# Output projections of a two-layer decoder trunk as seven block products, their block sums on GpSimd

## The chip, the core and the metric

The kernel runs on one core of a Trainium2 chip. A core has engines that run side by side, each with its own queue of instructions: TensorE (PE in the profile; its weight loads are the rows PEld) multiplies matrices, VectorE (DVE), ScalarE (ACT) and GpSimd (POOL) work element by element, and SyncE (SP) issues most of the transfers. An engine takes its instructions strictly in order; one that waits for a semaphore holds up all that stand behind it. SBUF is the on-chip memory of 128 partitions, PSUM the accumulator memory into which TensorE writes. The metric is the device time of one execution, in microseconds (us); lower is better.

## The reference

Two layers run over a sequence of 1024 positions, model width 1024, all in float32. Each has a token mixer (multi-head latent attention in layer 0, sliding-window attention in layer 1) beside four memory cross-attention heads, then one output projection, then a squared-ReLU MLP:

```python
def reference(x, mem, positions, ...):
    mem_n = rmsnorm(mem, mem_norm_g)
    for i in range(DEPTH):                       # DEPTH = 2
        hn = rmsnorm(x, attn_norm_g[i])
        if i % 2 == 0:
            mix, q_cross = mla_mixer(hn, positions, ...)      # 12 heads of 64
        else:
            mix, q_cross = swa_mixer(hn, positions, ...)      # 12 heads of 64
        cross = memory_cross_attention(q_cross, mem_n, w_mem_kv[i])   # 4 heads of 64
        x = x + jnp.concatenate([mix, cross], axis=-1) @ w_o[i]       # 1024x1024 @ 1024x1024
        x = x + squared_relu_mlp(rmsnorm(x, mlp_norm_g[i]), mlp_w_up[i], mlp_w_down[i])
    return rmsnorm(x, final_norm_g)
```

The line that ends in `@ w_o[i]` is what the change is about: a product of two 1024 x 1024 matrices in each layer, added to the residual `x`, whose row-wise RMS norm then feeds the MLP.

## The kernel before, in words

**Numbers.** Products are made of pairs: a float32 operand is split into a high part, which ScalarE copies with rounding (line 99), and a low part, the difference, which VectorE subtracts (line 100). A product of two such operands is three matmuls, high by high, high by low and low by high (`mm3`, lines 108 to 110). So each operand that TensorE is to use costs one ScalarE and one VectorE instruction first. A matmul takes a 128x128 block of stationary weights and 512 columns.

**The output projection.** `wo_phase` runs once in each layer, between the attention and the MLP. It works in two halves, output columns 0 to 511 and then 512 to 1023, and in each through eight tiles of 128 rows. A tile is eight 128-deep steps of three matmuls, 24 in all, into one PSUM bank `pswo`; so a layer has 2 x 8 x 24 = 384 of these matmuls. `WoHalf` loads and splits the weights of a half (`woq` of the first, `g` of the second), and `o_split` splits one row tile of the attention's output ahead of its use. The order is written out in the code: each engine gets its instructions in the order in which a tile's turn issues them, and a scheduler moves some of them by its own estimate of readiness.

**Behind each tile.** VectorE adds the bank to the residual (line 1294, one per tile and half). In the second half each tile is then stored to `xd` by two transfers on GpSimd's queue (line 1303), normed (`norm`: the squares on ScalarE at line 1150, five small operations on VectorE from line 1154 to 1159, then the scaled halves, one on ScalarE at line 1230 and one on VectorE at line 1231) and transposed by TensorE (`xT_`, line 1241) one tile later, between two tiles' matmuls. The transposed tile is split or copied for the MLP. For tiles 4 to 7 four subtractions on VectorE (lines 1248 to 1251) make the block combinations that the MLP needs, since both products of the MLP use the seven-product scheme already.

**Around it.** In layer 0 the attention's last head is divided by its sums in `last_o`: four reciprocals and four products on VectorE (lines 986 and 987) for each half of the rows. For rows 0 to 511 they are dealt out between the first four tiles. In layer 1 the sliding-window attention normalises its weights with GpSimd (line 1996). `fill_w` makes the first weights of the MLP: it scales them by the norm's gain on ScalarE, 128x128 at a time (line 1320), and splits them. In the MLP the matmuls that come first are named `psu` and `psv` (lines 1421 to 1423).

## Time and profile before

| what | value |
|---|---|
| median of 3 runs | 2111.34 us (2109.48 to 2112.94) |
| the profiled execution's own time | 2109.36 us |
| its span, first to last instruction | 2107.5 us |
| mean granted clock of TensorE | 0.999 |
| busy share PE, DVE, ACT, POOL | 99%, 70%, 53%, 7% |
| output projection of layer 0 | begins at 442.8 us, the MLP's first matmul at 538.3 us |
| output projection of layer 1 | begins at 1392.4 us, the MLP's first matmul at 1486.2 us |

The page of a profile gives busy times and shares, then groups of equal instructions. A row of the timeline is read as: start, duration, engine, line of the source, operation, written tile, read tiles, and in brackets how long the engine had been idle and what ended that. Two rows of one engine can overlap by about 0.1 us, since an instruction begins while the one ahead still drains; what an instruction costs in a full queue is the distance between two starts. Times in all parts are positions within this one execution.

### The profile page before, as it was taken

The page shows a single profiled execution, that of the slowest core. Times are in us where ns is not written, and L with a number is a line of the kernel's source. Part 1 is how long each engine was busy: PE and PEld are TensorE (multiplying, and loading weights), DVE is VectorE, ACT ScalarE, POOL GpSimd, SP SyncE. Part 2 cuts the span into 40 slices and gives each one's busy share as a digit, 9 for nine tenths or more (in the row PEclk, how much of TensorE's full clock was granted, in tenths as well). Part 3 has the DMA queues.
Part 4 walks back from the last instruction along what each step waited for, and adds up shares of the span by engine and source line. Part 5 has one row for each costly group of instructions (what it writes and reads, how often), then busy time and mean ns, then how long its engine had stood idle before and what let it go on. Part 6 is the DMA issues. An engine that isn't in the chain of part 4 may idle for free.

```text
span 2107.5 us, 28961 instructions
## 1 busy us (share of the span) xinstructions
PE 2082.1 (99%) x9830; PEld 1691.0 (80%) x9830; DVE 1476.6 (70%) x2929; ACT 1114.6 (53%) x2408; POOL 147.9 (7%) x248
## 2 busy tenths in 40 slices
PE   8999999999999999999999999999999999999998
PEld 7888766678888888888888878778788888888887
DVE  8766677775977776976557535666977776976565
ACT  7554466656755444444445435776755444444453
POOL 1001001010000000000001133420000000000000
PEclk9999999999999999999999999999999999999999
DMA  6202223343355446954433634542345446844342
GB/s 237 79 1 76 63 64 92 91 136 100 112 169 165 152 143 231 321 152 156 136 119 103 153 90 126 140 136 85 111 164 165 159 141 231 318 150 154 119 120 88
DMA packets 180756, 292.34 MB, mean 139 GB/s; under 512 B 16659, under 2 KB 70784, under 8 KB 180608
## 3 DMA queue, kind: packets, MB, share of 16 engines
q1 hardware_dynamic: 174096, 272.07, 41.4%
q0 software_dynamic: 5200, 15.80, 2.1%
q10 hardware_dynamic: 1312, 2.63, 0.4%
q8 instruction: 77, 1.26, 0.3%
q14 instruction: 71, 0.58, 0.1%
HBM read 187.34 MB, written 81.18 MB: 127 GB/s over the span
## 4 chain that ended last, share of the span: by engine, by line
PE 90%; DVE 5%; DMA 2%; ACT 2%; issue 1%; SPq 0%; DVEq 0%; ACTq 0%
PE psy L1730 5%; PE psy L1728 5%; PE psy L1729 5%; PE psu L1421 5%; PE psu L1422 5%; PE psu L1423 5%; PE psz L1728 4%; PE psz L1730 4%; PE psz L1729 4%; PE psv L1422 4%; PE psv L1421 4%; PE psv L1423 4%; PE pso L947 4%; PE pss L917 3%; PE pswo L108 3%; PE pswo L110 3%
## 5 line engine op out<-in xcount | busy, mean ns | idle before, releaser
L927 ACT ACTIVATE p<-pss 128x512 f32<-128x512 f32 (+2 forms) x144 | 68.7, 487 | 69.2 <-DVE pss L925 52.5
L1728 PE MATMUL psy<-g 128*128 128x512 f32 x256 | 99.9, 390 | 0.0
L1729 PE MATMUL psy<-g 128*128 128x512 f32 x256 | 99.6, 389 | 0.0
L1730 PE MATMUL psy<-g 128*128 128x512 f32 x256 | 99.4, 390 | 0.0
L99 ACT ACTIVATE g<-i 128x512 fp32r<-128x512 f32 x79 | 49.7, 629 | 92.5 <-PE psz L1729 46.0
L100 DVE TENSOR_TENSOR g<-i,g 128x512 fp32r<-128x512 f32 x79 | 55.6, 704 | 47.6 <-ACT g L99 47.6
L99 ACT ACTIVATE i<-mr 128x512 fp32r<-128x512 f32 x78 | 47.8, 628 | 74.0 <-PE psy L1729 25.6
L796 DVE TENSOR_REDUCE m<-psx 128x1 f32<-128x1024 f32 (+7 forms) x96 | 72.0, 752 | 20.1 <-PE psx L795 19.7
L99 ACT ACTIVATE uh<-i 128x512 fp32r<-128x512 f32 x66 | 41.7, 631 | 83.9 <-PE psy L1729 39.5
L947 PE MATMUL pso<-p,vf 128*128 128x512 f32 (+2 forms) x192 | 85.4, 527 | 0.6 <-ACT p L927 0.6
L100 DVE TENSOR_TENSOR uh<-i,uh 128x512 fp32r<-128x512 f32 x66 | 45.6, 690 | 46.8 <-ACT uh L99 46.6
L1728 PE MATMUL psz<-g 128*128 128x512 f32 x192 | 74.7, 389 | 0.0
L1729 PE MATMUL psz<-g 128*128 128x512 f32 x192 | 74.7, 389 | 0.0
L1730 PE MATMUL psz<-g 128*128 128x512 f32 x192 | 74.7, 389 | 0.0
L1320 ACT ACTIVATE mr<-mr,gcol 128x256 f32<-128x256 f32 (+1 forms) x160 | 63.9, 475 | 13.5 <-DMA mr<-in_mlp_w_up_dram 13.5
L100 DVE TENSOR_TENSOR i<-mr,i 128x512 fp32r<-128x512 f32 x78 | 53.6, 687 | 21.5 <-ACT i L99 21.5
L917 PE MATMUL pss<-qh,kh 97*128 97x512 f32 (+2 forms) x144 | 67.9, 474 | 0.0
L917 PE MATMUL pss<-ql,kh 97*128 97x512 f32 (+2 forms) x144 | 58.2, 404 | 0.0
L1641 DVE TENSOR_TENSOR mqf<-mqq,mqf 128x512 f32<-128x512 f32 x64 | 43.4, 688 | 20.6 <-DMA mqq<-in_mlp_w_down_dram 20.3
L1730 PEld LDWEIGHTS psy<-g 128*128 128x128 f32 x256 | 48.1, 188 | 10.0
L1729 PEld LDWEIGHTS psy<-g 128*128 128x128 f32 x256 | 48.1, 188 | 9.9
L1728 PEld LDWEIGHTS psy<-g 128*128 128x128 f32 x256 | 48.1, 188 | 9.8
(658 smaller groups left out, 6862.2 us busy)
## 6 DMA issues: line engine op xcount, KB each, us to landing
i<-hd SPq DMA_DIRECT2D x154, 256.0 KB
hd<-uh SPq DMA_DIRECT2D x76, 256.0 KB
hd<-ul SPq DMA_DIRECT2D x76, 256.0 KB
mr<-in_mlp_w_up_dram SPq DMA_DIRECT2D x36, 512.0 KB
hd<-x SPq DMA_DIRECT2D x72, 256.0 KB
mr<-hd SPq DMA_DIRECT2D x70, 256.0 KB
d<-in_mlp_w_up_dram SPq DMA_DIRECT2D x32, 512.0 KB
mqq<-in_mlp_w_down_dram SPq DMA_DIRECT2D x32, 512.0 KB
```

The lines of the kernel that those rows point to most:

```text
L99: nc.scalar.activation(hi, src, AF.Copy)
L100: nc.vector.tensor_tensor(lo, src, f32(hi), ALU.subtract)
L796: nc.vector.reduce_max(m8s[h][:, i : i + 1], ps[:, :n], axis=AX, negate=True)
L917: return lambda: nc.tensor.matmul(o, a, b, skip_group_check=True, **kw)
L927: nc.scalar.activation(p[:, c0:], ps, AF.Exp, scale=SC)
L947: mms.append(lambda: nc.tensor.matmul(o, a, b, skip_group_check=True, **kw))
L1421: nc.tensor.matmul(ps, wh[:, k, :], xh[:, k, :], start=p in (1, 2, 5) and k == 0, stop=False, skip_group_check=True)
L1422: nc.tensor.matmul(ps, wh[:, k, :], xl[:, k, :], start=False, stop=False, skip_group_check=True)
L1423: nc.tensor.matmul(ps, wl[:, k, :], xh[:, k, :], start=False, stop=k == 3, skip_group_check=True)
L1728: nc.tensor.matmul(ps, ah[:, j, :], bh, start=p in (1, 5, 2) and k == 0, stop=False, skip_group_check=True)
L1729: nc.tensor.matmul(ps, ah[:, j, :], bl, start=False, stop=False, skip_group_check=True)
L1730: nc.tensor.matmul(ps, al[:, j, :], bh, start=False, stop=k == NP - 1, skip_group_check=True)
```

## The change

A class `Wo` takes the place of `WoHalf`. The attention output A (rows by heads) and the weights B are cut into 2 x 2 blocks of 512: A12 is rows 0 to 511 by the early heads, B21 the weights of the early heads by columns 0 to 511, and so on. Seven block products are made in the order 2, 1, 5, 6, 3, 7, 4:

```text
P2 = A12 B21            P5 = (A21+A22) (B12-B11)     P6 = (A21+A22-A11) (B22-B12+B11)
P1 = A11 B11            P3 = (A12-A21-A22+A11) B22   P7 = (A11-A21) (B22-B12)
P4 = A22 (B21-B22+B12-B11)
```

Each is 4 row tiles x 4 steps x 3 = 48 matmuls. Some products continue in a bank (6 and 7 on top of 1; 3 on top of 5), and VectorE adds the banks to four residual blocks `a1`, `u2`, `c21`, `a5` of 512 x 512 (line 1324 of the new source): 36 additions in a layer, where there were 16.

Every product needs four A blocks and four B blocks of 128x512 split anew, into a ring of eight operand sets (`set_`). The sums and differences of blocks are GpSimd instructions of 128x512 (`sums`, lines 765 to 776): 8 for P5, 8 for P6, 4 for P3, 8 for P7 and 4 for P4, 32 in a layer. Also given to GpSimd are one half of the norm's scaling (line 1293, 8 in a layer, ScalarE before), the gain scaling in `fill_w` (line 1400, 2 of 128x1024 in a layer for 16 small ones on ScalarE) and the subtractions for tiles 4, 5 and 6 (lines 1312 to 1315, 12 in a layer; tile 7's stay on VectorE).

P2 needs the early heads only, and its matmuls are put among the last steps of the attention, in eight pieces of six (`first`). In layer 0 `last_o` for rows 0 to 511 is issued whole, ahead of P1's operands. Residuals and weights come in transfers of 1 MB, and the four result blocks leave in one transfer each on SyncE's queue, where there were 32 smaller ones on GpSimd's. Rows 0 to 511 are complete when P3 is added, so their norms stand among P3 and P7 and their transposes among P7; rows 512 to 1023 are complete with P4, the last product, so the norms of tiles 4 to 7 follow P4's tiles, and the transposes of tiles 6 and 7 stand in the MLP's first product.

**GpSimd's queue, layer 0.** Before, it had only the issues of transfers here (`xd` is the result in DRAM, `i..` the tiles), then, much later, a weight scaling of the next layer. The last three of those issues and what follows:

```order
L1303 DMA xd_4796<-i32_0_49_5320 128x512
L1303 DMA xd_4796<-i30_0_53_5382 128x512
L1303 DMA xd_4796<-i31_0_60_5458 128x512
L1841 TENSOR_TENSOR wsr1_9773<-wsr1_9773,gcol_73 128x1024
L1699 DMA x1_4795<-d2_0_152_7966 128x512 x2
```

Now the stretch holds the sums (`ul` and `uh` are the sum blocks of A and B, `fa1` and `qn0` the attention's output, `x0`, `x1`, `x2` the weight blocks B12, B22, B21). From the second half of P7's sums to the subtractions of tile 4 the rows run:

```order
L773 TENSOR_TENSOR fa1_87<-fa1_87 128x512
L774 TENSOR_TENSOR x0_0_2_4883<-x1_0_3_4885,x0_0_2_4883 128x512
L776 TENSOR_TENSOR uh_0_17_4917<-x2_0_4_4887,uh_0_17_4917 128x512 x2
L776 TENSOR_TENSOR uh_0_18_4918<-x2_0_4_4887,uh_0_18_4918 128x512 x2
L1400 TENSOR_TENSOR mr_0_31_5301<-mr_0_31_5301,gcol_73 128x1024
L1400 TENSOR_TENSOR mr_0_34_5308<-mr_0_34_5308,gcol_73 128x1024
L1293 TENSOR_SCALAR d3_0_28_5220<-g0_0_1_4881,cosb_74 128x512
L1293 TENSOR_SCALAR d4_0_29_5247<-g0_0_1_4881,cosb_74 128x512
L1293 TENSOR_SCALAR d3_0_30_5274<-g0_0_1_4881,cosb_74 128x512
L1293 TENSOR_SCALAR d4_0_39_5331<-g0_0_1_4881,cosb_74 128x512
L1293 TENSOR_SCALAR d3_0_42_5460<-g3_0_23_4925,cosb_74 128x512
L1312 TENSOR_TENSOR x0_0_40_5348<-x1_0_45_5526,x0_0_40_5348 128x4x128
```

Behind P4's sums (`uh` from `x2`) stand the two weight scalings, the norm scaling of five tiles and the first subtraction, all in the one queue.

**VectorE's queue, layer 0, between the first two products.** Before, there were splits of attention tiles and of weights, and one addition per tile:

```order
L100 TENSOR_TENSOR x2_0_23_5029<-qn0_1958,x2_0_23_5029 128x512
L100 TENSOR_TENSOR x2_0_23_5029<-fa1_87,x2_0_23_5029 128x512
L100 TENSOR_TENSOR g2_0_26_5094<-wor0_1_2_4984,g2_0_26_5094 128x1024
L100 TENSOR_TENSOR d0_0_34_5140<-qn0_1958,d0_0_34_5140 128x512
L1294 TENSOR_TENSOR i7_0_7_4862<-pswo0_0_7_4951,i7_0_7_4862 128x512
L100 TENSOR_TENSOR x3_0_25_5064<-qn0_1958,x3_0_25_5064 128x512
L100 TENSOR_TENSOR x3_0_25_5064<-fa1_87,x3_0_25_5064 128x512
```

Now P2's additions to `g0` (block `a1`) are followed by P5's operands, whose low parts are taken from GpSimd's sum blocks `ul` and `uh`, ahead of P1's additions:

```order
L1324 TENSOR_TENSOR g0_0_1_4881<-pso0w2_2_4832,g0_0_1_4881 128x512
L1324 TENSOR_TENSOR g0_0_1_4881<-pso0w2_3_4846,g0_0_1_4881 128x512
L100 TENSOR_TENSOR woq0_0_4408<-ul_0_19_4919,woq0_0_4408 128x512 x2
L100 TENSOR_TENSOR woq0_0_4408<-uh_0_17_4917,woq0_0_4408 128x512 x2
L100 TENSOR_TENSOR woq0_1_4486<-ul_0_20_4920,woq0_1_4486 128x512
L100 TENSOR_TENSOR woq0_1_4486<-uh_0_18_4918,woq0_1_4486 128x512
L100 TENSOR_TENSOR woq0_1_4486<-ul_0_20_4920,woq0_1_4486 128x512
L100 TENSOR_TENSOR woq0_1_4486<-uh_0_18_4918,woq0_1_4486 128x512
L1324 TENSOR_TENSOR g0_0_1_4881<-pso0w1_0_4943,g0_0_1_4881 128x512
L1324 TENSOR_TENSOR g0_0_1_4881<-pso0w1_1_4961,g0_0_1_4881 128x512
```

So VectorE's splits of P5 can't begin until GpSimd has the sums, and P1's additions stand behind them.

**TensorE's queue, end of layer 0's projection.** Before, tile 5's transposes (`psT_m0_5`) were followed by the 24 matmuls of the last row tile, of which the first and the last are shown here, and only tiles 6 and 7 were left for the MLP's first product `psu0_0`:

```order
L1241 MATMUL psT_m0_5_0_5567<-ident_63,d4_0_63_5494 128x128 x4
L1241 MATMUL psT_m0_5_1_5573<-ident_63,d4_0_63_5494 128x128 x4
L108 MATMUL pswo0_1_7_5584<-g0_0_13_4944,d1_0_67_5524 128x512
...
L110 MATMUL pswo0_1_7_5584<-g2_0_26_5094,d2_0_68_5551 128x512
L1421 MATMUL psu0_0_5648<-mqq0_0_30_5134,uh_0_47_5307 128x512
L1422 MATMUL psu0_0_5648<-mqq0_0_30_5134,uh_0_47_5307 128x512
L1241 MATMUL psT_m0_6_0_5622<-ident_63,d3_0_69_5557 128x128 x4
L1241 MATMUL psT_m0_6_1_5628<-ident_63,d3_0_69_5557 128x128 x4
```

Now the transposes of tiles 4 and 5 stand directly ahead of the MLP's first matmul, with nothing between:

```order
L799 MATMUL pso0w4_3_5539<-woq0_1_4486 128x512
L800 MATMUL pso0w4_3_5539<-woq0_1_4486 128x512
L801 MATMUL pso0w4_3_5539<-woq0_1_4486 128x512
L1304 MATMUL psT_m0_4_5521<-ident_63,d3_0_42_5460 128x128 x8
L1304 MATMUL psT_m0_5_5564<-ident_63,d4_0_43_5485 128x128 x4
L1493 MATMUL psu0_0_5590<-mqq0_0_37_5315,uh_0_32_5302 128x512
L1494 MATMUL psu0_0_5590<-mqq0_0_37_5315,uh_0_32_5302 128x512
L1495 MATMUL psu0_0_5590<-mqq0_0_37_5315,ul_0_33_5303 128x512
L1304 MATMUL psT_m0_5_5564<-ident_63,d4_0_43_5485 128x128 x4
L1493 MATMUL psu0_0_5590<-mqq0_0_37_5315,uh_0_32_5302 128x512
```

In the new order the inputs of these transposes, `d3` and `d4`, are written half by GpSimd and half by VectorE from the last product's results, whose last matmul is a few rows above.

The diff, cut to the operands, sums and products, the phase itself, and the places in the attention and the MLP that it calls from:

```diff
+    class Wo:
+        ORD = (2, 1, 5, 6, 3, 7, 4)
...
+        def a(self, q, k):
+            kt = (self.early if q % 10 == 2 else self.late)[k]
+            return self.o[kt // 4][:, kt % 4, halves[q // 10 - 1]]
...
+        def sides(self, n):
+            p, k = self.ORD[n // 4], n % 4
+            q = {2: (12, 21), 1: (11, 11), 3: (12, 22), 7: (11, 12), 4: (22, None)}.get(p)
+            if q is None:
+                return self.b1[k], self.c1[k]
+            return self.a(q[0], k), self.blk[q[1]][k] if q[1] else self.c1[k]
+        def prep_b(self, n):
+            st = self.set_(n)
+            split(self.sides(n)[1], st[2], st[3])
+        def prep_a(self, n):
+            st = self.set_(n)
+            split(self.sides(n)[0], st[0], st[1])
+            self.ops[n] = st
+        def prep(self, n):
+            self.prep_a(n)
+            self.prep_b(n)
+        def sums(self, p):
+            G = nc.gpsimd.tensor_tensor
+            A, B, b1, c1 = self.a, self.blk, self.b1, self.c1
+            for k in range(4):
+                if p == 5:
+                    G(b1[k], A(21, k), A(22, k), ALU.add)
+                    G(c1[k], B[12][k], B[11][k], SUB)
+                elif p == 6:
+                    G(b1[k], b1[k], A(11, k), SUB)
+                    G(c1[k], B[22][k], c1[k], SUB)
+                elif p == 3:
+                    G(A(12, k), A(12, k), b1[k], SUB)
+                elif p == 7:
+                    G(A(11, k), A(11, k), A(21, k), SUB)
+                    G(B[12][k], B[22][k], B[12][k], SUB)
+                else:
+                    G(c1[k], B[21][k], c1[k], SUB)
...
+        def mm(self, ip, j, ks=range(4)):
+            p = self.ORD[ip]
+            ps = self.bank(p, j)
+            c = slice(j * P, (j + 1) * P)
+            for k in ks:
+                ah, al, bh, bl = self.ops[4 * ip + k]
+                ah, al = ah[:, c], al[:, c]
+                nc.tensor.matmul(ps, ah, bh, start=p in (1, 2, 4, 5) and k == 0, stop=False, skip_group_check=True)
+                nc.tensor.matmul(ps, ah, bl, start=False, stop=False, skip_group_check=True)
+                nc.tensor.matmul(ps, al, bh, start=False, stop=k == 3, skip_group_check=True)
+        def first(self):
+            for j in range(4):
+                for ks in ((0, 1), (2, 3)):
+                    self.mm(0, j, ks)
+                    yield
...
-                if G:
-                    last_o(G, at.tile([64, 512], F32, tag="on", bufs=2, name="rq1"))
+                last_o(G, at.tile([64, 512], F32, tag="on", bufs=2, name=f"rq{G}"))
...
-    wq = WoHalf(0, 0, quad_slots())
+    wo0 = Wo(0, [f0, f1])
+    wo_first = wo0.first()
+    wo_at = {109: lambda: wo0.raw_pair(21), 127: lambda: wo0.raw_pair(11)}
+    for k, (nb, na) in enumerate(((115, 124), (118, 129), (121, 133), (124, 139))):
+        wo_at.setdefault(nb + 0.5, lambda k=k: wo0.prep_b(k))
+        wo_at.setdefault(na + 0.25, lambda k=k: wo0.prep_a(k))
...
             next(muls, None)
-        if n >= 9 * NB + 8 and n % 3 == 0:
-            wq.step()
+        for e in (0, 0.25, 0.5):
+            if n + e in wo_at:
+                wo_at[n + e]()
+        if n >= len(seq):
+            next(wo_first)
...
+        def norm(t, done=()):
+            y = ys[t] = m.t(f"d{3 + t % 2}")
...
             rs = rst.pop(t).get()
-            nc.scalar.activation(y[:, 0, :], xa[t], AF.Copy, scale=rs)
-            nc.vector.tensor_scalar(y[:, 1, :], xb, rs, None, ALU.mult)
...
+            nc.gpsimd.tensor_scalar(y[:, 0, :], xs[0], rs, None, ALU.mult)
+            nc.vector.tensor_scalar(y[:, 1, :], xs[1], rs, None, ALU.mult)
...
+                G = (nc.vector if t == NT - 1 else nc.gpsimd).tensor_tensor
                 r = [xr[i][:, :, c] for i in range(4)]
                 m.t2[j] = t2 = k4(m.t(f"i{2 * j}")[:, 0, :])
-                nc.vector.tensor_tensor(r[0], r[1], r[0], SUB)
-                nc.vector.tensor_tensor(t2, r[3], r[0], SUB)
-                nc.vector.tensor_tensor(r[1], r[3], r[1], SUB)
-                nc.vector.tensor_tensor(r[2], r[2], t2, SUB)
+                G(r[0], r[1], r[0], SUB)
+                G(t2, r[3], r[0], SUB)
+                G(r[1], r[3], r[1], SUB)
+                G(r[2], r[2], t2, SUB)
...
+        to = {1: ("a1",), 2: ("a1",), 5: ("a5",), 6: ("u2",), 3: ("u2",), 7: ("a5", "c21"), 4: ("c21",)}
+        def add(ip, j):
+            ps = wo.bank(wo.ORD[ip], j)
+            for nm in to[wo.ORD[ip]]:
+                d = acc[nm][:, j, :]
+                nc.vector.tensor_tensor(d, ps, d, ALU.add)
...
+        for n in range(4, 8):
+            wo.prep(n)
...
+        if layer == 0:
+            residual("c21", "g3", 1, 0)
+        for j in range(4):
+            add(0, j)
+        if layer == 0:
+            new_psum(2)
+        wo.sums(5)
+        for ip in range(1, 7):
+            p = wo.ORD[ip]
+            if p == 7:
+                for k in range(4):
+                    wo.prep(4 * ip + 4 + k)
+                for i in range(2):
+                    m.fill.append(fill_w(layer, m, i))
+                flip[0] += 1
                 for i in range(2):
                     q = m.quad(f"q{i}", F32R)
                     X[i + 1] = [q[:, 0:4, :], q[:, 4:8, :]]
-        m.last_T = lambda: xT_(NT - 1)
+            for j in range(4):
+                wo.mm(ip, j)
+                if ip < 5:
+                    wo.prep(4 * ip + 4 + j)
+                add(ip, j)
+                if p == 5:
+                    half(j, 0, m.t(f"d{3 + j % 2}")[:, 0, :])
+                if p == 3:
+                    if j:
+                        norm(j - 1, (0,))
+                if p == 7:
+                    if j == 0:
+                        norm(3, (0,))
+                    xT_(j)
+                if p == 4:
+                    norm(4 + j)
+                    if j > 1:
+                        xT_(2 + j)
+            if p == 1:
+                store("a1", 0, 0)
+                wo.sums(6)
+            if p == 5:
+                for q in (3, 7):
+                    wo.sums(q)
+            if p == 6:
+                wo.sums(4)
+            if p == 3:
+                store("u2", 0, 1)
+            if p == 7:
+                store("a5", 1, 1)
+        store("c21", 1, 0)
+        m.lateT = [lambda: xT_(NT - 2), lambda: xT_(NT - 1)]
...
         nc.sync.dma_start(out=raw, in_=mlp_w_up[layer].rearrange("(k p) f -> p k f", p=P)[:, :, 256 * i : 256 * i + P])
-        scale_w(layer, raw, 0)
+        nc.gpsimd.tensor_tensor(raw, raw, g_mlp[layer].unsqueeze(2).to_broadcast([P, KT, P]), ALU.mult)
         split(raw, wh, wl)
...
         load_raw(0)
         go(0, 1, m.fill[0][1])
-        m.last_T()
+        m.lateT[0]()
         go(0, 2, m.fill[0][2])
+        m.lateT[1]()
...
     for _ in swa:
-        wq.step()
-    while wq.todo:
-        wq.step()
+        n += 1
+        next(wo_at, lambda: None)()
+        if len(su) - 12 - n < 5:
+            next(wo_first, None)
+    for f in wo_at:
+        f()
+    for _ in wo_first:
```

More of the change, by code (lines that the diff above doesn't have):

```diff
@@ L706, in quad_slots, with k4, k512 @@
[L706 to L719 removed]
+    SUB = ALU.subtract
+    def k4(ap):
+        return ap.rearrange("p (k c) -> p k c", k=4)
+    def k512(ap):
+        return ap.rearrange("p a (b c) -> p (a b) c", c=512)
@@ L2106, in trunk @@
     kv1p.release()
-    m1 = Mlp(1, x1)
-    wo_phase(1, wq, o1, m1)
+    m1 = Mlp(1, x1, xnp1)
+    wo_phase(wo1, m1)
     mlp(1, m1)
```

235 lines of the change are left out of this document (92 added, 143 removed).

## The prediction

> **What bounds the kernel now.** I read the page's busy shares and its chain first, then the two projections as windows, then TensorE's timeline at their edges.
>
> ```profile
> PE 2082.1 (99%) x9830; PEld 1691.0 (80%) x9830; DVE 1476.6 (70%) x2929; ACT 1114.6 (53%) x2408; POOL 147.9 (7%) x248
> PE 90%; DVE 5%; DMA 2%; ACT 2%; issue 1%; SPq 0%; DVEq 0%; ACTq 0%
> ```
>
> TensorE is busy for 99% of the span and makes up 90% of the chain: work taken from it is time won, if the other engines still feed it. Whether they do is a matter of the stages. The next rows are the projections of layers 0 and 1 and the first 52 to 54 us of the MLP behind each (stretch, length, then busy us per engine).
>
> ```profile
> 442.80:538.30 95.50, 94.13 (x439) 77.42 (x438) 68.50 (x137) 61.65 (x137) 8.17 (x15) 1.00 0.36 119
> 1392.40:1486.20 93.80, 93.58 (x441) 77.77 (x441) 62.59 (x122) 63.61 (x135) 8.20 (x15) 1.00 0.39 127
> 538.30:590.00 51.70, 51.09 (x233) 41.87 (x232) 49.71 (x88) 36.76 (x75) 0.54 (x1) 1.00 0.43 147
> 1486.20:1540.00 53.80, 53.27 (x236) 42.97 (x235) 49.70 (x86) 37.74 (x77) 0.54 (x1) 1.00 0.44 147
> ```
>
> In the projections TensorE lacks 1.4 and 0.2 us; VectorE (the third number, 68.5 and 62.6) has some 27 to 31 us free, GpSimd nearly everything. Right behind, VectorE is busy for 49.7 of 51.7 and of 53.8 us: it has 2 and 4 us to give there, in both layers. That is the stage to watch. The gaps of TensorE are small:
>
> ```profile
> 445.24 0.33 PE L947 MATMUL pso<-ph,vh 128*128 128x128 f32 x1 [0.70 <-ACT ph L99]
> 539.49 1.09 PE L1241 MATMUL psT_m<-ident,d 128*128 128x128 f32 x8 [0.61 <-ACT d L1230]
> 1485.31 1.09 PE L1241 MATMUL psT_m<-ident,d 128*128 128x128 f32 x8 [0.22 <-ACT d L1230]
> ```
>
> and the chain at layer 1's edge, read in order of time (start, length, what), already runs over VectorE, one instruction of 0.60 after another, until TensorE's transposes take over:
>
> ```profile
> 1479.17 0.60 DVE i L1294
> 1479.77 0.60 DVE mqf L100
> 1480.37 0.60 DVE x L1248
> ...
> 1484.53 0.73 ACT d L1230
> 1485.26 0.04 issue
> 1485.31 0.67 PE psT_m L1241 x4
> ```
>
> So anything that holds VectorE up here reaches TensorE with almost no slack.
>
> **What is removed.** One row tile of the old scheme is 24 matmuls:
>
> ```profile
> 483.62 0.39 PE L110 MATMUL pswo<-woq,x 128*128 128x512 f32 x1
> ...
> 489.06 0.39 PE L110 MATMUL pswo<-woq,x 128*128 128x512 f32 x1
> ```
>
> (489.06 - 483.62) / 24 = 0.2267 us each. A layer goes from 384 to 7 x 48 = 336, so 48 x 0.2267 = 10.9 us less, **-21.8 us** in both. Transposes stay 64 a layer. That the products are really fewer can be counted in the order, 672 against 768; a rival in which TensorE's work doesn't shrink is out.
>
> **Prices of what is added.** The rows nearest to the new instructions:
>
> ```profile
> L1996 POOL TENSOR_TENSOR sp<-sp,sst 128x768 f32<-128x768 f32 x28 | 42.0, 1501 | 29.3 <-DVE sst L1995 29.2
> L1841 POOL TENSOR_TENSOR wsr<-wsr,gcol 128x1024 f32<-128x1024 f32 x12 | 22.9, 1905 | 346.9 <-DMA wsr<-in_swa_w_in_dram 301.8 <-DVE fb L103 25.7 <-DVE g L100 19.4
> L1950 POOL CAST df<-di 128x256 f32<-128x256 int32 x7 | 3.9, 552 | 0.5
> L1996 POOL TENSOR_TENSOR sp<-sp,sst 128x384 f32<-128x384 f32 x4 | 3.3, 830 | 19.3 <-DVE sst L1995 18.2 <-PE psw L1972 1.0
> L986 DVE RECIPROCAL rq<-pso 64x128 f32<-64x128 f32 x4 | 3.8, 960 | 0.1
> ...
> 1501.92 0.69 DVE L100 TENSOR_TENSOR d<-d,d 128x512 fp32r<-128x512 f32 x1
> 1502.52 0.69 DVE L100 TENSOR_TENSOR mqf<-x,mqf 128x512 fp32r<-128x512 f32 x1
> ```
>
> A sum of 128x512 on GpSimd lies between 0.83 (384 columns) and 1.50 (768). On the line from 384 to 1024 columns, (1.905 - 0.830) / 640 = 1.68 ns a column, it is 0.83 + 128 x 0.00168 = 1.05 us; I take that. A norm scaling there has one large input; the nearest row is the cast of 256 columns, 0.55, so 0.55 to 1.10, and I take 0.8. A VectorE instruction of 512 columns costs 0.60 in a full queue (1502.52 - 1501.92).
>
> The Trainium skill, page "GPSIMD Engine Reference", section "4.1 Engine selection", speaks against the move: two-input elementwise work belongs on VectorE, GpSimd being about half as fast. From VectorE's 0.69 that would be an estimate of 1.38 for a sum of 512; with it the projection's 64 sums would add another 21 us at most to the result below. The rows of 830 and 1905 decide for 1.05.
>
> **The two engines get in each other's way.** This carries the forecast. Rows of GpSimd and VectorE at four places:
>
> ```profile
> 815.88 1.90 POOL L1841 TENSOR_TENSOR wsr<-wsr,gcol 128x1024 f32<-128x1024 f32 x1 [275.64 <-DMA wsr<-in_swa_w_in_dram]
> 815.94 2.39 DVE L1361 TENSOR_TENSOR d<-d,d 128x512 f32<-128x512 f32 x1
> 818.26 0.68 DVE L1362 TENSOR_TENSOR d<-d 128x512 f32<-128x512 f32 x1
> 1117.25 1.98 POOL L1841 TENSOR_TENSOR wsr<-wsr,gcol 128x1024 f32<-128x1024 f32 x1 [1.79 <-DMA wsr<-in_swa_w_in_dram]
> 1117.39 2.12 DVE L1710 TENSOR_SCALAR i<-g,sinb 128x512 f32<-128x512 f32 x1
> 1119.43 0.47 DVE L1710 TENSOR_SCALAR i<-d,sinb 128x512 f32<-128x512 f32 x1
> 1363.19 1.47 POOL L1996 TENSOR_TENSOR sp<-sp,sst 128x768 f32<-128x768 f32 x1
> 1363.03 0.53 DVE L2008 COPY spT<-pswt 128x384 f32<-128x384 f32 x1
> 1363.47 2.27 DVE L100 TENSOR_TENSOR woq<-wor,woq 128x1024 fp32r<-128x1024 f32 x1
> 193.29 0.60 POOL L312 TENSOR_TENSOR fa<-fa,ra 128x192 f32<-128x192 f32 x1 [56.02 <-DVE ra L309]
> 193.57 0.61 DVE L103 SCALAR_TENSOR_TENSOR wqnl<-wr,gcol,wqnh 128x256 fp32r<-128x256 f32 x1
> 193.85 0.78 POOL L313 TENSOR_TENSOR fa<-fa,rb 128x192 f32<-128x192 f32 x1
> ```
>
> A subtraction that takes 0.68 by itself takes 2.39 when it starts 0.06 us after a GpSimd instruction of 1.90: it ends 0.55 after that one's end. The scaling of 0.47 takes 2.12 in the same way. The copy out of PSUM at 1363.03 isn't held. And when both have a queue they take turns: at 193 us VectorE's instruction gets in between two of GpSimd's, and the second of these waits. So I count VectorE instructions with both large inputs in SBUF, and its scalings from SBUF, as excluded by any GpSimd instruction, and additions out of PSUM (the 36 of line 1324) as free.
>
> The Trainium skill, "GPSIMD Engine Reference", section "1. Specifications", says the same of the SBUF interfaces: shared, with contention for VectorE instructions in a two-port mode or with two SBUF inputs. The trace agrees, 2.39 for 0.68.
>
> **The feeding of the products.** From the start of P5's sums to the last operand of P4 the shared path must take 32 sums x 1.05 = 33.6 and the low parts of six products, 48 x 0.60 = 28.8: 62.4 us. TensorE wants P4's operands after five products, 5 x 10.9 = 54.4. The lack is 8.0; and one sum, the copy (a 0.6 like VectorE's) and the subtraction of the first operands add 1.05 + 0.6 + 0.6 = 2.2 that nothing hides. So TensorE stands some 10.2 us in each projection, where it stood 1.4 and 0.2: **+8.8 and +10.0**. The additions of a product stand behind the next product's splits on VectorE, so late sums also keep banks; I give that nothing, since three of the seven products go on in a bank they hold. Bounds: with no exclusion only the start is left, about 1 a layer; with sums at 1.50 the path takes 76.8 and the lack is 22.4.
>
> last_o in one piece puts four reciprocals of 0.96 with their products ahead of P1's splits in layer 0; eight pieces of P2 (six matmuls, 1.4 us each), of which some are still to come, cover about as much: 0, and 3.7 if the cover is gone, inside the bounds above.
>
> **The change of stage.** From P7 on GpSimd has two weight scalings of 1.9, eight norm scalings of 0.8 and twelve subtractions of 1.05: 3.8 + 6.4 + 12.6 = 22.8 us. In layer 0's order, between those weights' splits and the third MLP product, 33 of VectorE's 55 large instructions read SBUF alone, so about 0.6 x 22.8 = 13.7 us of its queue is held. It loses the twelve subtractions, -7.2, and gets twelve additions where three stood near the end before, +5.4. Sum 13.7 - 1.8 = 11.9, and the rows of 49.7 in 51.7 and 53.8 say that VectorE has 2 to 4 to take it with; but the transposes of tiles 4 and 5 now stand directly ahead of the MLP and wait for both engines, where a tile of 24 matmuls (5.4 us) lay between before. I let the one cancel the other: **+12 a layer, +24**. Bounds: 5 without exclusion (8 of the subtractions at 1.05 for 0.60 in a row, 3.6, and the additions), 16 with none of the slack and the norms at 1.10.
>
> **What costs nothing.** P2's matmuls are moved, not added; the gap of 0.70 in the attention's tail could take one in, worth that much at most. ScalarE gets more copies but has 32 of 95 us free and loses the gain scalings. The four stores and the loads of 1 MB go to SyncE's queue, whose DMA engines are busy for 0.36 to 0.39 here; nobody waits for the stores. GpSimd loses 32 issues.
>
> **The sum.** -21.8 + 18.8 + 24.0 = +21.0. The profiled execution took 2109.4, so 2130.4 against its own time; it is 2.0 under the median of 2111.3, and on the median it is 2132. I forecast **2131**. About 0.2%, 4 us, is what a measurement of this kernel can tell from no change.
>
> **Rivals.**
> - *No exclusion, gain mostly kept (faster).* The sums run while VectorE works on PSUM additions and small norm steps, and the turns fall well. For it: GpSimd is idle for 87 of 95 us now, and 22 of 55 large instructions of VectorE aren't held. Against it: every overlapping pair above is held. It decides if less than about half of the held time reaches TensorE. -21.8 + 2 + 10 = -9.8: 2101.
> - *All of it is gained.* -21.8: 2089. It needs slack behind the projection, and there are 2 to 4 us.
> - *Only one of the two places binds.* If only the feeding, -21.8 + 18.8 = -3.0: 2108; if only the change of stage, -21.8 + 24 + 2 = +4.2: 2115.
> - *GpSimd is the bound all the way.* Sums dearer than 1.05 or turns that go to it: feeding 15 a layer, stage change 16: -21.8 + 30 + 32 = +40: 2151.
>
> **How the numbers follow.** The forecast, 2118 to 2144, 0.60; GpSimd as the bound 0.10; one place only 0.12, half of it within 0.2%; gain mostly kept 0.14; all gained 0.04. Slower is 0.60 + 0.10 + 0.05 = 0.75, no change 0.07, faster 0.14 + 0.04 = 0.18. The range goes to the one side to 2098, a little past the kept gain, to the other to 2150: outside are the full gain, a part of the kept gain and half of the dearest case, 0.15 to 0.2.
>
> **What would show it.** In the new profile: GpSimd's 512-column sums near 1.05, and near 1.6 where a subtraction stands before them; VectorE's line 100 mean well above 0.69 in both projections; TensorE idle about 10 us within each projection, ended by line 99 or 100 and by sums, and again about 12 at the MLP's start, ended by the norm scalings and subtractions of GpSimd or by VectorE behind them. It is wrong if TensorE is busy throughout while GpSimd and VectorE overlap at full length, or if those gaps are half as long.

## The result and the profile after

The changed kernel takes 2180.14 us (median; 2178.35 to 2180.27), the kernel before, beside it, 2110.56 us (2109.48 to 2112.94): a ratio of 1.0326 (1.0308 to 1.0344), or +69.6 us, where +20 had been forecast. Since TensorE has 21.8 us less to do, 69.6 + 21.8 = 91.4 us of new lost time have to be found. The profiled execution took 2180.22 us, its span 2178.5 us, its mean granted clock 0.983 (before 0.999).

From the page of the changed kernel: TensorE's and its neighbours' busy time, the chain that ended last, and TensorE's granted clock in 40 slices.

```profile
PE 2088.1 (96%) x9734; PEld 1685.4 (77%) x9734; DVE 1548.5 (71%) x2969; ACT 1103.9 (51%) x2392; POOL 305.9 (14%) x324
PE 84%; DVE 7%; POOL 3%; issue 2%; DMA 2%; ACT 2%; SPq 0%; POOLq 0%; DVEq 0%; ACTq 0%
PEclk9999999989899999999999999989899999999999
```

TensorE has 96 matmuls fewer (9734 for 9830) and is nevertheless busy for longer, 2088.1 us for 2082.1: some of its matmuls have become slower. The digits 8 of the clock lie, in each layer, at the start of the projection and again at the change of stage to the MLP. Layer 0 shows both losses. The windows of the changed kernel, with the columns of the prediction (stretch, length, busy time of PE, PEld, DVE, ACT, POOL, then granted clock, DMA share, GB/s); the first two stretches are those shown of before:

```profile
442.80:538.30 95.50, 74.86 (x314) 58.94 (x313) 84.56 (x114) 39.28 (x80) 56.99 (x36) 0.89 0.34 112
538.30:590.00 51.70, 35.69 (x155) 27.18 (x154) 40.38 (x77) 35.12 (x81) 29.69 (x18) 0.87 0.19 68
480.00:490.00 10.00, 0.00 (x0) 0.00 (x0) 10.00 (x8) 3.40 (x8) 10.00 (x7) 0.57 0.51 145
490.00:495.00 5.00, 4.27 (x10) 3.40 (x11) 1.75 (x3) 0.00 (x0) 5.00 (x4) 0.50 0.52 130
```

In the same 95.5 us TensorE does 314 matmuls instead of 439. For ten of them it does nothing at all while VectorE and GpSimd are both busy throughout, and in the five that follow it runs at half its clock. Its waits by cause (total, times, longest):

```profile
PE psT_m L1304 <- POOL d L1293: 20.5, 12, 3.1
PE pso0w L799 <- DVE g L1324: 14.6, 2, 12.7
PE pso1w L799 <- DVE g L1324: 8.8, 1, 8.8
PE psu L1493 <- ACT mqf L99: 8.1, 2, 4.0
PE pso0w L800 <- DVE i L100: 4.4, 2, 2.4
```

Between 440 and 600 us TensorE is idle for 36.6 us (2.0 before), and in the corresponding stretch of layer 1 for 30.9 (0.7 before): 64.8 us more. Matmuls that start over 0.3 us after the one ahead, with no idle time in between, add 10.2 and 12.9 us over the usual 0.227 (1.2 and 1.4 before): 20.5 us more. The two make 85.3 of the 91.4 us.

By place, TensorE's idle time ahead of the products' matmuls (the feeding) is 20.4 us in layer 0 and 15.5 in layer 1, where it was 1.4, the attention's tail included, and nothing. Ahead of the transposes and of the MLP's matmuls, some 50 us of them (the change of stage), it is 16.2 and 15.4, where it was 0.6 and 0.7. So both places lose, the feeding 34.5 and the change of stage 30.3 us of idle time.

The longest wait, on TensorE's timeline of the changed kernel:

```profile
477.66 0.39 PE L801 MATMUL pso0w<-woq 128*128 128x512 f32 x1
490.73 0.80 PE L799 MATMUL pso0w<-woq 128*128 128x512 f32 x1 [12.69 <-DVE g L1324]
491.33 0.63 PE L800 MATMUL pso0w<-woq 128*128 128x512 f32 x1
491.75 0.63 PE L801 MATMUL pso0w<-woq 128*128 128x512 f32 x1
...
495.16 0.40 PE L800 MATMUL pso0w<-woq 128*128 128x512 f32 x1
495.40 0.39 PE L801 MATMUL pso0w<-woq 128*128 128x512 f32 x1
```

The stalled matmul is the first of P5's second row tile; it waits for an addition of line 1324, and after the stall matmuls begin 0.42 us apart (491.75 - 491.33) until 495. What VectorE and GpSimd did in that time, on their timelines (same kernel):

```profile
478.46 1.59 DVE L100 TENSOR_TENSOR i<-ul,i 128x512 fp32r<-128x512 f32 x1 [0.78 <-ACT i L99]
479.97 1.75 DVE L100 TENSOR_TENSOR i<-uh,i 128x512 fp32r<-128x512 f32 x1
481.65 1.75 DVE L100 TENSOR_TENSOR i<-ul,i 128x512 fp32r<-128x512 f32 x1
...
488.34 1.74 DVE L100 TENSOR_TENSOR d<-ul,d 128x512 fp32r<-128x512 f32 x1
490.00 0.68 DVE L1324 TENSOR_TENSOR g<-pso0w,g 128x512 f32<-128x512 f32 x1
```

```profile
447.82 5.03 POOL L765 TENSOR_TENSOR ul<-fa,qn 128x512 f32<-128x512 f32 x4 [20.52 <-DVE fa L1104]
...
481.14 3.39 POOL L771 TENSOR_TENSOR qn<-qn,ul 128x512 f32<-128x512 f32 x2
484.49 1.71 POOL L773 TENSOR_TENSOR fa<-fa 128x512 f32<-128x512 f32 x1
486.16 1.71 POOL L774 TENSOR_TENSOR x<-x,x 128x512 f32<-128x512 f32 x1
...
496.57 5.50 POOL L776 TENSOR_TENSOR uh<-x,uh 128x512 f32<-128x512 f32 x4
502.03 4.65 POOL L1400 TENSOR_TENSOR mr<-mr,gcol 128x1024 f32<-128x1024 f32 x2
521.00 1.86 POOL L1293 TENSOR_SCALAR d<-g,cosb 128x512 f32<-128x512 f32 x1 [14.32 <-DVE cosb L1249]
```

GpSimd's sums alone take 5.03 / 4 = 1.26 us each. Here it is already at the sums of P3 and P7 (lines 771, 773, 774), which nobody needs yet, while VectorE splits P6's operands (`ul`, `uh`), which TensorE needs next. The two take turns: VectorE's splits start 1.68 us apart (481.65 - 479.97), and the addition, which frees the bank that TensorE waits for, stands behind seven splits and one other addition. By 502.1 all sums are done and by 506.7 the two weight scalings, and GpSimd stands idle for 14.32 us: the shortage is not spread over the projection but sits early. Of the 20.4 us, 18.5 are lost before P6's first matmul.

### The profile page after: what moved, and what is told of

Same layout as the page of the kernel before. It is cut to its first block, busy times and chain, and to the rows that moved or that the text cites. A ratio compares the mean times of both kernels' runs of the same rounds, so it can differ in the third digit from the quotient of the medians.

```text
span 2178.5 us, 28842 instructions
## 1 busy us (share of the span) xinstructions
PE 2088.1 (96%) x9734; PEld 1685.4 (77%) x9734; DVE 1548.5 (71%) x2969; ACT 1103.9 (51%) x2392; POOL 305.9 (14%) x324
## 3 DMA queue, kind: packets, MB, share of 16 engines
q10 hardware_dynamic: 1312, 2.63, 0.4%
## 4 chain that ended last, share of the span: by engine, by line
PE 84%; DVE 7%; POOL 3%; issue 2%; DMA 2%; ACT 2%; SPq 0%; POOLq 0%; DVEq 0%; ACTq 0%
PE psy L1801 5%; PE psy L1803 5%; PE psy L1802 5%; PE psu L1494 5%; PE psu L1495 5%; PE psu L1493 5%; PE pso L1036 4%; PE psz L1803 4%; PE psz L1802 4%; PE psz L1801 4%; PE psv L1493 4%; PE psv L1495 4%; PE psv L1494 4%; PE pss L1006 3%; PE psf L108 2%; PE psf L110 2%
## 5 line engine op out<-in xcount | busy, mean ns | idle before, releaser
L885 DVE TENSOR_REDUCE m<-psx 128x1 f32<-128x1024 f32 (+7 forms) x96 | 71.8, 751 | 20.8 <-PE psx L884 20.4
L1914 POOL TENSOR_TENSOR wsr<-wsr,gcol 128x1024 f32<-128x1024 f32 x12 | 23.4, 1951 | 343.1 <-ACT i L99 270.8
L1714 DVE TENSOR_TENSOR mqf<-mqq,mqf 128x512 f32<-128x512 f32 x64 | 43.1, 684 | 23.8 <-DMA mqq<-in_mlp_w_down_dram 23.5
```

The costliest lines, as they stand in the source:

```text
L885: nc.vector.reduce_max(m8s[h][:, i : i + 1], ps[:, :n], axis=AX, negate=True)
```

## The experiments

The theory at first was that GpSimd's sums hold VectorE up and that TensorE waits for what stands behind; the rivals put the loss elsewhere, on the order of the additions, on VectorE's own load, on the late pieces on GpSimd. Each expectation names what it weighs. Since several causes sat in one stretch, the runs first take them out one by one and then put the sums back into a kernel free of the others. All ratios are to the kernel before, whose median beside them was 2109.5 to 2111.3 us.

**The order of the additions.** P5's and P3's banks come in pairs, one tile of two banks, and the second row tile's first matmul waited for VectorE's addition out of the first bank of the same tile. Here both row tiles are made before both additions.

```diff
-                add(ip, j)
+                if p not in (5, 3):
+                    add(ip, j)
+                elif j % 2:
+                    add(ip, j - 1)
+                    add(ip, j)
```

> The changed kernel, with the additions of P5 and P3 issued behind both row tiles of a two-bank accumulator instead of behind each tile. In the changed kernel the second tile's matmuls of P5 wait 12.7 and 8.8 us for the addition that reads the first tile in the same two-bank tile, and that addition stands on VectorE behind six splits of P6. Theory A (the operands are late: GpSimd's sums and VectorE's splits share one path, and P6's operands come at the same late time in any case): only the remaining matmuls of P5, 30 x 0.227 = 6.8 us a layer, move into the wait, so some 2165 us, 12 to 16 less than 2180. Theory B (the accumulator is what holds, and operands would be there): both waits and the slow clock behind them (about 2 us each) go, 2155 or less.

2175.64 us, ratio 1.0304 (1.0274 to 1.0334): 4.5 us less than the changed kernel, which is neither number, and the intervals of the two ratios overlap. Its waits:

```profile
PE psT_m L1304 <- POOL d L1293: 21.3, 13, 5.7
PE psu L1497 <- ACT mqf L99: 10.8, 2, 5.4
PE pso1w L800 <- DVE d L100: 5.7, 4, 2.4
```

The waits of 12.7 and 8.8 us for line 1324 are gone, and most of the time comes back behind them: TensorE waits for P6's operands themselves and for the norms of the next stage. Idle time falls by 14.0 us in the feeding and grows by 6.9 at the change of stage. A stall that hides others is not worth its length.

**The sums on VectorE.** All 64 go from GpSimd to VectorE's own queue.

```diff
-            G = nc.gpsimd.tensor_tensor
+            G = nc.vector.tensor_tensor
```

> The changed kernel with all 64 block sums on VectorE instead of GpSimd, nothing else moved. Theory A (exclusion and dear sums: 1.26 us each on GpSimd alone, 1.7 in turns, during which VectorE's splits stand): a sum costs 0.60 in its place, the path of one projection falls from 32 x 1.26 + 28.8 = 69 us to 48 plus VectorE's free additions, and the time falls by 20 to 30, to 2150 to 2160. Theory B (VectorE's own work is the bound and GpSimd's sums are beside it): 64 x 0.60 = 38 us come on top in the projections, 2200 to 2218.

2168.66 us, ratio 1.0271 (1.0241 to 1.0301), 11.5 us less; between the two numbers expected, and nearer to the lower. The longest wait for an addition falls to 4.8 us. VectorE with 64 more instructions is faster than VectorE with GpSimd at its side, but only by a little; the wait for norm scalings on GpSimd grows from 20.5 to 26.1 us in all.

**No sums.** The products take blocks as they are, so that 64 instructions and their waits vanish and nothing else does.

```diff
-            for k in range(4):
+            self.b1 = [A(21, k) for k in range(4)]
+            self.c1 = [B[12][k] for k in range(4)]
+            for k in ():
```

> The changed kernel with the 64 block sums left out: the products take unsummed blocks, so the projections compute something else; splits, products and additions stay. It measures all that the sums cost in the projection. Theory A (the sums are what makes operands late): the idle time of TensorE inside the projections falls from 18.5 and about 15.5 us to under 5 each, with 2 to 5 us a layer of slow clock; 2180 - 30 to 40 = 2140 to 2150, and what is left above 2089 is the change of stage. Theory B (VectorE's splits and additions alone can't feed seven products): less than 15 us are won.

2123.30 us, ratio 1.0061 (1.0038 to 1.0084): 56.8 us less, more than either theory had. The sums, in whatever way they cost, are most of the loss.

**The late pieces.** The norm scaling and the gain scaling go back to ScalarE, the subtractions of tiles 4 to 6 to VectorE; GpSimd keeps the sums. A second kernel puts back the norm scaling alone (the first line of the diff).

```diff
-            nc.gpsimd.tensor_scalar(y[:, 0, :], xs[0], rs, None, ALU.mult)
+            nc.scalar.activation(y[:, 0, :], xs[0], AF.Copy, scale=rs)
...
-                G = (nc.vector if t == NT - 1 else nc.gpsimd).tensor_tensor
+                G = nc.vector.tensor_tensor
...
-        nc.gpsimd.tensor_tensor(raw, raw, g_mlp[layer].unsqueeze(2).to_broadcast([P, KT, P]), ALU.mult)
+        scale_w(layer, raw, 0)
```

> The changed kernel with the three late pieces taken from GpSimd again: the norm's scaling on ScalarE, the subtractions of tiles 4 to 6 on VectorE, the gain scaling of the first weights on ScalarE; the block sums stay on GpSimd. Theory A (GpSimd's queue and the exclusion make the change of stage): TensorE's idle time of 16.2 us from P7 to the third MLP product of layer 0 falls to 5 or less, in layer 1 the same, and the slow clock there goes: 2180 - 25 to 35 = 2145 to 2155. Theory B (rows 512 to 1023 come complete only with the last product, so norms and transposes stand bare whoever does them): under 12 us are won.

> The changed kernel with one of the three late pieces moved back alone: the 16 norm scalings go to ScalarE, the subtractions and the gain scaling stay on GpSimd. On GpSimd such a scaling takes 1.6 to 2.5 us, and TensorE's waits name it with 20.5 us in all. Theory A (that scaling is the wait at the change of stage): most of the 24.5 us of the run that moved all three comes, 2160 to 2165. Theory B (the twelve subtractions in the same queue hold VectorE and the third MLP product): less than 10, 2171 or more, and the wait moves to them.

All three: 2155.65 us, ratio 1.0210 (1.0180 to 1.0239), 24.5 us less, just above theory A's range; the idle time at the change of stage falls from 16.2 and 15.4 us to 7.6 and 8.0, not to 5. The norm scaling alone: 2165.48 us, ratio 1.0256 (1.0227 to 1.0286), 14.7 us less, just above theory A's range too. So the norm scaling is 14.7 of the 24.5. Its price on GpSimd, in the groups of the changed kernel between 440 and 600 us (busy, mean ns):

```profile
L1293 POOL TENSOR_SCALAR d<-g,cosb 128x512 f32<-128x512 f32 x5 | 9.7, 1931 | 38.0 <-DVE cosb L1249 31.0 <-ACT d L1240 7.1
L1293 POOL TENSOR_SCALAR d<-g,sinb 128x512 f32<-128x512 f32 x3 | 6.4, 2126 | 0.2 <-DVE sinb L1249 0.2
```

and on ScalarE, in the kernel with the norm scaling there (515 to 600 us):

```profile
L1293 ACT ACTIVATE d<-g,cosb 128x512 f32<-128x512 f32 x5 | 3.6, 721 | 0.0
L1293 ACT ACTIVATE d<-g,sinb 128x512 f32<-128x512 f32 x3 | 2.2, 728 | 2.8 <-DVE sinb L1249 2.8
```

1.9 to 2.1 us for 0.72, and directly ahead of the transposes that TensorE waits for. The times on GpSimd are those beside VectorE's work, not of GpSimd alone.

**Sums that nobody reads.** To part the waiting for sums from the disturbance by sums, GpSimd again does 64 sums of the same blocks at the same places, and the products take blocks as they are.

```diff
-                    G(A(12, k), A(12, k), b1[k], SUB)
+                    G(b1[k], A(12, k), b1[k], SUB)
...
-                    G(A(11, k), A(11, k), A(21, k), SUB)
-                    G(B[12][k], B[22][k], B[12][k], SUB)
+                    G(b1[k], A(11, k), A(21, k), SUB)
+                    G(c1[k], B[22][k], B[12][k], SUB)
```

> The kernel without sums (products take unsummed blocks, so the projections compute something else), but GpSimd does the 64 sums all the same, at the same places, into tiles that nobody reads. No engine waits for a sum any more; only the two engines' meeting is left. The kernel without sums has 2123, the changed one 2180. Theory A (exclusion): 32 sums x 1.26 = 40 us lie side by side at the start of each projection, the 25 to 30 splits that fall into them take 1.7 instead of 0.6, 25 to 30 us of VectorE's queue a layer, and TensorE loses 10 to 20 of it: 2143 to 2163. Theory B (only the dependence on a late sum costs): 2123 to 2128.

2183.57 us, ratio 1.0342 (1.0312 to 1.0372), as slow as the changed kernel and outside what was expected. This run decides nothing. Its longest waits of TensorE are

```profile
PE pso1w L804 <- DVE g L1329: 18.7, 1, 18.7
PE psT_m L1309 <- POOL d L1298: 17.2, 8, 5.1
PE pso0w L804 <- DVE g L1329: 11.6, 2, 10.2
```

and ScalarE stands 17.78 us behind a sum of line 781 in layer 1: the unread sums went into the tiles `ul` and `uh`, whose next users waited for them, and GpSimd's own late pieces stood behind them too. So this had to be made again on a kernel without those links.

**The ladder without the late pieces.** The next four kernels have both edits above, the additions behind both row tiles and the late pieces off GpSimd. They differ in the sums alone: on VectorE; left out; on GpSimd and unread, in one tile of their own; on GpSimd and read.

```diff
+                unread = self.s_
+                if p in (5, 6, 7):
+                    G(unread, A(11, k), A(21, k), SUB)
+                    G(unread, B[22][k], B[12][k], SUB)
+                elif p == 3:
+                    G(unread, A(12, k), A(11, k), SUB)
+                else:
+                    G(unread, B[21][k], B[12][k], SUB)
```

> The seven products with nothing new on GpSimd: block sums and subtractions on VectorE, norm and gain scaling on ScalarE, and P5's and P3's additions behind both tiles of a two-bank accumulator. If the gains add up: 2180 - 11.5 - 24.5 - 4.5 = 2140, and VectorE is busy nearly all the time in both projections, which then is the bound that is left. If they are the same time won twice: 2148 to 2156. Under 2111 would need VectorE to have the room for 64 x 0.60 = 38 us, which it has not.

> As the one before, with the block sums left out altogether (the products take unsummed blocks, so the projections compute something else): the seven products at their best, if sums cost nothing. If splits and additions feed TensorE: near the full gain of 21.8, 2089 to 2096. If the 36 additions, the 56 splits and the norms of rows 512 to 1023 behind the last product still bind at the change of stage: 2100 to 2112, a few us of idle time behind P4 in each layer.

> The kernel of 2107 (no sums, late pieces off GpSimd, additions behind both tiles; products take unsummed blocks, so the projections compute something else), with 64 sums of the same shape on GpSimd, all written to one tile that nobody reads. No scaling, no weight tile and no store stands behind them, as they did in the run before with unread sums. What is added is only GpSimd at work beside VectorE. Theory A (exclusion): each of 32 sums holds VectorE's SBUF instructions for about 1.07 us while both have a queue; 24 to 30 splits of a layer meet one, 26 to 32 us later on VectorE, less some slack, with slow clock behind the stalls: 2107 + 40 to 60 = 2147 to 2167. Theory B (what cost was scalings and tiles waiting behind sums): under 2117.

> The changed kernel with the late pieces off GpSimd and the additions behind both tiles; the 64 sums stay on GpSimd and are read. It differs from the run with unread sums (2147) only in that operands wait for their sums, and from the one with all on VectorE (2131) only in who makes the sums. Theory A (exclusion is nearly all that a sum on GpSimd costs): 2147 to 2152. Theory B (waiting for late sums costs much on top): 2153 to 2156, no more, since the run with the late pieces alone moved back has 2156.

| sums | us (median) | ratio (interval) |
|---|---|---|
| left out | 2107.07 | 0.9980 (0.9968 to 0.9991) |
| on VectorE | 2130.53 | 1.0091 (1.0062 to 1.0120) |
| on GpSimd, unread | 2147.04 | 1.0179 (1.0149 to 1.0208) |
| on GpSimd, read | 2148.99 | 1.0183 (1.0153 to 1.0212) |

Three of the four came out as one of their theories had it. With all on VectorE it is 10 us less than the gains added up to (2140). That GpSimd works beside VectorE costs 2147.0 - 2107.1 = 40.0 us, though nobody waits for a single result: no wait of any engine in that trace names a line of the sums, and TensorE's two largest are for VectorE's splits:

```profile
PE pso1w L799 <- DVE woq L100: 5.9, 5, 2.4
PE pso0w L799 <- DVE i L100: 5.7, 2, 4.0
```

Read or unread, the sums on GpSimd differ by 2 us, which the intervals don't tell apart. The groups of VectorE between 447 and 495 us, first with the sums left out, then unread on GpSimd (busy us, mean ns), with the window 447 to 492 us of each:

```profile
L1326 DVE TENSOR_TENSOR g<-pso0w,g 128x512 f32<-128x512 f32 x16 | 10.4, 683 | 3.0 <-issue 1.5 <-PE pso0w L803 1.5
L100 DVE TENSOR_TENSOR woq<-x,woq 128x512 fp32r<-128x512 f32 x8 | 5.2, 682 | 0.0
...
447.00:492.00 45.00, 42.48 (x179) 34.02 (x179) 38.87 (x63) 30.40 (x67) 0.00 (x0) 0.96 0.53 176
```

```profile
L100 DVE TENSOR_TENSOR woq<-x,woq 128x512 fp32r<-128x512 f32 x4 | 6.9, 1774 | 0.0
L1323 DVE TENSOR_TENSOR g<-pso0w,g 128x512 f32<-128x512 f32 x8 | 5.0, 676 | 0.0
...
447.00:492.00 45.00, 34.38 (x133) 26.18 (x132) 43.38 (x42) 19.40 (x42) 37.26 (x25) 0.85 0.40 138
```

The splits of line 100, whose two inputs are in SBUF, go from 0.68 to 1.77 us in the group shown, and to between 0.95 and 1.77 in the other groups of 128x512 in this stretch; the additions that read PSUM stay at 0.68. In the same 45 us VectorE gets 42 instructions done instead of 63, with 43.4 us of it recorded as busy.

With the sums on VectorE the exclusion is gone, and VectorE itself is, by its busy time, the limit. The window of that kernel:

```profile
454.00:554.00 100.00, 87.38 (x371) 67.23 (x370) 95.16 (x192) 70.10 (x157) 0.00 (x0) 0.91 0.30 100
```

VectorE works 95.2 of 100 us. 64 x 0.60 = 38 us of sums cost 23.5 us of time.

The steps add up in one order:

| step | us | from |
|---|---|---|
| before, less 96 matmuls | 2088.8 | 2110.6 - 21.8 |
| more splits and additions, norms behind the last product | +18.3 | sums left out |
| GpSimd working beside VectorE | +40.0 | unread against left out |
| waiting for the sums | +2, not told apart from 0 | read against unread |
| additions of a pair of banks | +6.7 | 2155.65 - 2148.99 |
| late pieces on GpSimd | +24.5 | 2180.14 - 2155.65 |

The sizes belong to this order. The first edit is worth 4.5 us with the late pieces still on GpSimd and 6.7 without them; both times the intervals of the ratios overlap, so that its size is uncertain by a few us. No version that makes the sums beats the kernel before; even with sums that cost nothing it would gain only 0.2%.

## Why the prediction was wrong

The sign was right, the size was not: +69.6 us against +20, and outside the range.

- **The removed matmuls.** 96 fewer, as counted. This step held.
- **The feeding of the products, forecast 18.8, measured 40 + 2 + 6.7 = 48.7 by the steps, and 34.5 of idle time by place, without the slow matmuls** (of the 40, 5.6 are idle time at the change of stage). This is the step that failed. Its mechanism was the right one: the splits are excluded by GpSimd's sums, PSUM additions are not, and a turn of one sum and one split was counted as 1.05 + 0.60 = 1.65 where 1.68 is measured. The sum alone takes 1.26, not 1.05; the rows it was drawn through were scalings with a broadcast second operand (lines 1841 and 1996), and those are cheaper. The Trainium skill, page "GPSIMD Engine Reference", section "3.1 Elementwise — side-by-side cycle accounting", has 2.6 cycles an element for two inputs, at 1.2 GHz an estimate of 1.11 us for 512 before any start-up. The trace's 1.26 is above that estimate and the 1.05 taken was under it; how much of the 1.26 is start-up no run here shows.

  But this price isn't what failed: in a turn a sum adds only 1.68 - 0.60 = 1.08, so 32 of them move the path's 62.4 by 1 us. What failed was to set the whole work till P4 against the whole time till P4. The two engines share by turns, not by need, so sums for P3 and P7 took turns from P6's splits; TensorE had lost its time by P6, and the later idleness of GpSimd (14.32 us) didn't give it back. Eight of those sums start before VectorE's last split for P6 (490.60); at 1.08 each that is an estimate of 9 us of the stall of 12.69. This is read from the timelines: no run put those sums later.
- **"The additions of a product stand behind the next product's splits on VectorE, so late sums also keep banks; I give that nothing."** It was worth some 4.5 to 6.7 us, and in the changed kernel it was the longest stall. That three products go on in a bank they hold was true and beside the point: the stalled matmul opened a new bank, which shared a tile with the one being added.
- **The change of stage, forecast 24, measured 24.5 for the late pieces and 30.3 of idle time in all.** That 24 and 24.5 are so near is luck, since they aren't the same thing. The forecast was for the whole stage, with the additions in it and the bare transposes set against VectorE's slack; the 24.5 are only what the late pieces cost on GpSimd. In the kernel without sums and late pieces 10.3 us of idle time still stand there (before 1.3), so the 24.5 aren't the whole of it. Within the 24.5 the norm scaling was priced at 0.8 us from a cast, and takes 1.57 to 2.53 beside VectorE's work; it makes 14.7, and the other late pieces, by difference, 9.8.
- **What was costed at nothing or nearly so.** With no exclusion "only the start is left, about 1 a layer"; the kernel without sums and late pieces loses 18.3. By the timelines of that kernel idle time is 7.8 and 5.0 us in the two layers (before 2.0 and 0.7), 10.2 more, and matmuls without idle time ahead that start over 0.3 us apart cost 4.5 and 4.8 (before 1.2 and 1.4), 6.7 more: together 16.9 of the 18.3. Of the 10.2, 9.0 stand at the change of stage and 1.1 in the feeding; how much there is due to the bare transposes, how much to the additions and how much to the late norms wasn't taken apart. The additions are 32 in a layer (that many rows of line 1324 in each layer of the trace), not the 36 counted ahead of the result; as they were held to be free, no sum changes by it.
- **The clock.** The forecast had no term for it. Matmuls that start late without idle time ahead make 20.5 of the 91.4 us, spread over all the steps above; 79 of them start 0.42 to 0.44 us after the one ahead, as in the stretch from 490 to 495 us, where the granted clock is 0.50, and these alone lose some 16 us.
- **The rivals.** "GpSimd is the bound all the way" (2151) came nearest in time but isn't what happened: GpSimd waits 14.32 and later 13.53 us for norms in layer 0. "No exclusion" is refuted by the 40 us, and "only one of the two places" by the idle time of 35.9 us in the feeding and 31.6 at the change of stage.
- **What was to show it.** Sums near 1.05 was wrong; near 1.6 behind a subtraction, right (1.71); line 100 well above 0.69, right. The gaps are about twice what was named in layer 0's projection (20.4 us for 10; 15.5 in layer 1), and 16.2 and 15.4 from P7 to the MLP's start for 12. The longest waits within the projections were ended by additions (line 1324), not by line 99 or 100.

## What to carry to other kernels

Work given to GpSimd isn't free because GpSimd is idle: if it reads SBUF beside VectorE's two-input SBUF instructions, count each pair as nearly the sum of both (here 1.68 us for 1.26 and 0.60), and find the moment when urgent work takes turns with work that could wait, since that moment sets the loss and not the total. An algorithm that saves one multiplication in eight pays for itself only if its extra splits, sums and additions fit into VectorE's slack: here 21.8 us of TensorE were bought with 18.3 us even before any sum was made, and half of that is idle time at the change of stage behind the last product. When several waits stand in one stretch, don't read a stall's length as its worth; take the causes out together, then put them back one at a time.

## What the runs showed of the hardware

- GpSimd takes 1.57 to 2.53 us to scale 128x512 by one number per partition (line 1293, 16 times in the changed kernel), while ScalarE takes 0.72. Beside all 16 VectorE has scalings, splits or subtractions at work, so these aren't times alone; whether this form with one large input is cheaper by itself than a sum of two (1.26 alone) no run shows.
- TensorE's clock fell to half after several short stalls. In the kernel with the sums left out:

```profile
455.84 0.50 PE L801 MATMUL pso0w<-i,i 128*128 128x512 f32 x1 [1.53 <-ACT i L99]
457.11 0.50 PE L802 MATMUL pso0w<-i,i 128*128 128x512 f32 x1 [0.76 <-DVE i L100]
...
458.31 0.79 PE L802 MATMUL pso0w<-i,i 128*128 128x512 f32 x1 [0.23 <-DVE i L100]
458.90 0.63 PE L803 MATMUL pso0w<-i,i 128*128 128x512 f32 x1
459.33 0.63 PE L801 MATMUL pso0w<-d,d 128*128 128x512 f32 x1
```

Three stalls, of 1.53, 0.76 and 0.23 us, are followed by matmuls 0.43 us apart (459.33 - 458.90) until 461.8; in the changed kernel the same follows stalls of 1.94 and 2.42 us, from 459.8 to 464.5. The granted clock is 0.51 in both stretches. The Trainium skill, page "TensorE: Matmul & The Clock Gate", section "What's actually happening", has the half clock come after at least one idle window of about 3.4 us; here no stall ahead of the fall was that long. What decides instead, perhaps the idle share of a stretch, wasn't tried. The same section of the Trainium skill has full speed return after some 3.4 us of steady work, which agrees roughly with the rows, 3.5 to 4.7 us.
